# A list scheduler's durations, hand-over delays and two new rules, in a planned network kernel on one core

## The chip, the cores and the metric

The kernel runs on one core of a Trainium2 chip. The metric is the device time of one execution in microseconds. Engine names in the profile: PE is TensorE's matmuls and PEld its weight loads, DVE is VectorE, ACT is ScalarE, POOL is GpSimd, SP is SyncE, whose queue issues most loads.

## The reference, cut to what matters

A network of three layers on 512 tokens of width 1024, with a context of 256 tokens in the first two. A layer of the first block:

```python
mx = jnp.split((jax.nn.silu(c) @ w_ada[l] + b_ada[l])[:, None, :], 6, axis=-1)
hx = modulate(rmsnorm(x, g_pre_mix[l]), mx[0], mx[1])
hc = modulate(rmsnorm(ctx, g_pre_mix[l]), mc[0], mc[1])
out_x, out_c = token_mixers(hx, hc, w_in[l], w_out[l], ...)
x = x + mx[2] * rmsnorm(out_x, g_post_mix[l])
hx = modulate(rmsnorm(x, g_pre_mlp[l]), mx[3], mx[4])
x = x + mx[5] * rmsnorm(sq_relu_mlp(hx, w_mlp1[l], w_mlp2[l]), g_post_mlp[l])
```

`token_mixers` runs a chunked mLSTM in both directions, a Fourier mixer and a convolution module side by side; `sq_relu_mlp` is `jnp.square(jax.nn.relu(h @ w1)) @ w2` with a hidden width of 4096. Context tokens take the same way in layer 0. A third layer with sparse attention, pooling and a memory follows. All is float32.

## The kernel before, in words

Activations stand with channels on the partitions and tokens in the columns: 768 columns in layer 0 (tiles of 512 and 256), 512 in layer 1. A float32 product is made of three fast ones: the weights are split into a rounded high part `wh` (ScalarE, from the raw weights `wr`) and the rest `wl` (VectorE), the activations likewise, and TensorE adds high*high, high*low and low*high in a PSUM tile `pd`. Weights stream from HBM in blocks of 512 KB. `w_ada`, which gives the modulation vectors, goes straight from `wr` through small products into `pa`. The MLP uses Strassen's scheme for most of its products: `combos` (line 1270) makes sums and differences T1 to T4 of the quarters of the activations, on VectorE and POOL, as `tmp`; `fast` (line 1486) uses them, `plain` (line 1479) does a tile without them, and `product2` (line 1475) is the second matrix. A hidden tile is squared by `square_parts` (line 1439): ScalarE takes relu into `ftmp` and the square's rounded part into a `slot`, POOL the full square into `ftmp`, and VectorE subtracts, `slot<-ftmp,slot`, for the low part. In layer 0 the program is `plain` for four column blocks, `combos`, then `product2` and `fast` in turn, seven times.

The program does not issue instructions itself. It is written to a `Recorder` (class at line 136), which notes each one with its engine, operands and dependences. All of them appear in the profile on one line, L395 in `issue`, so a tile's name tells what an instruction is. `schedule` (line 247) then goes through a model of time. An engine that is free takes, of the instructions that are ready, the one written first (some are marked urgent by a number), if its buffers can be had. Buffers are rings: 23 of `slot`, 6 of `tmp`, 4 of `ftmp`, 3 of `wr`, 2 each of `wh` and `wl`, 3 of `pd`, 4 of `pm`, 1 of `pa`. How long an instruction takes in the model is told by `cost` (line 212), and when the next may follow by constants in `schedule`:

```python
SEM, SLACK, SAME = 120.0, 300.0, {"pe": 0.0, "act": 120.0, "vec": 130.0, "pool": 60.0, "sp": 0.0}
...
wait = SAME[e] if same else SEM + (SLACK if ops[j].eng == "pe" else 0)
ready_at[j] = max(ready_at[j], o.end + wait)
```

The result is one fixed order for each engine and each queue. On the chip an engine runs its order strictly: an instruction that has to wait keeps back all that stands behind it on that engine, and a load on SP that waits for its buffer keeps back the loads behind it.

## Time and profile before

| | |
|---|---|
| median of 3 runs | 1974.14 us (1968.65 to 1974.84) |
| profiled execution, its own time | 1975.36 us |
| its span, first to last instruction | 1973.6 us |
| mean granted TensorE clock | 0.98 |
| TensorE busy | 1890.9 us, 96% |
| VectorE busy | 1354.0 us, 69% |
| ScalarE busy | 908.9 us, 46% |
| POOL busy | 425.8 us, 22% |

Busy shares are means over stages with different limits. Since TensorE is busy nearly always, the table says little more than where not to look; what a change of order can alter is in the few stretches in which TensorE stands still, and there the rows by time tell which engine it waited for. In those rows a number in brackets is the idle time just before an instruction and the engine and tile that ended it. Several equal instructions in a row are told as one with a count.

### The profile page before, as it was taken

What the parts mean: (1) busy time and instruction counts of PE and PEld (TensorE: products, weight loads), DVE (VectorE), ACT (ScalarE), POOL (GpSimd) and SP (SyncE); (2) the same over time, 40 slices, a digit from 0 to 9 for tenths busy, and PEclk for the clock granted to TensorE, in tenths of its full rate; (3) what the DMA queues carried; (4) which work ended last, traced back from release to release, by engine and by line L of the source; (5) the groups of instructions that cost most, each with busy time, mean ns of one, the idle gap of its engine ahead of it and who ended that gap; (6) DMA issues with size and microseconds to landing.
All of it is one profiled execution on the core that took longest, in us unless ns stands there. A gap on an engine that the chain in (4) does not pass through costs nothing.

```text
span 1973.6 us, 32415 instructions
## 1 busy us (share of the span) xinstructions
PE 1890.9 (96%) x12772; PEld 1641.0 (83%) x12772; DVE 1354.0 (69%) x2370; ACT 908.9 (46%) x1786; POOL 425.8 (22%) x438
## 2 busy tenths in 40 slices
PE   5999998998999999999989999889999999999999
PEld 3978886787888999999978888778989889888777
DVE  6499768368356556665677968577787778657686
ACT  4532256564323322332573345655334347556554
POOL 1110042215112211221301023233232221111321
PEclk8999999898999999999999999899999999999999
DMA  8233235243233112211361123352323244311121
GB/s 312 90 110 108 96 109 177 68 150 107 96 118 126 65 56 75 76 65 54 108 216 68 54 86 140 107 171 81 112 86 116 98 137 162 109 54 44 46 84 65
DMA packets 82714, 207.47 MB, mean 105 GB/s; under 512 B 8961, under 2 KB 36865, under 8 KB 82562
## 3 DMA queue, kind: packets, MB, share of 16 engines
q1 hardware_dynamic: 66114, 188.86, 28.0%
q10 hardware_dynamic: 16448, 16.54, 2.5%
q8 instruction: 100, 1.64, 0.3%
q14 instruction: 52, 0.43, 0.1%
HBM read 189.12 MB, written 16.25 MB: 104 GB/s over the span
## 4 chain that ended last, share of the span: by engine, by line
PE 80%; DVE 11%; ACT 3%; DMA 2%; issue 2%; POOL 1%; SPq 0%; DVEq 0%; POOLq 0%; ACTq 0%
PE pd L395 57%; PE pm L395 21%; DVE slot L395 7%; PE pa L395 3%; DVE tmp L395 2%; ACT slot L395 1%; DVE wl L395 1%; DMA wr<-in_w_ada 1%; DVE small L395 1%; ACT tmp L395 1%; DMA wr<-in_w_in 1%; ACT small L395 1%; DMA slot<-in_w_ada 1%; ACT wh L395 0%; DVE ftmp L395 0%
## 5 line engine op out<-in xcount | busy, mean ns | idle before, releaser
L395 PE MATMUL pd<-slot,wh 128*128 128x256 f32 (+2 forms) x4384 | 1092.2, 340 | 14.5 <-DVE slot L395 5.5
L395 PEld LDWEIGHTS pd<-slot,wh 128*128 128x128 f32 (+1 forms) x4384 | 744.7, 189 | 122.0 <-issue 17.5
L395 PE MATMUL pd<-slot,wl 128*128 128x256 f32 (+1 forms) x2136 | 720.9, 339 | 4.9 <-DVE wl L395 4.7
L395 PEld LDWEIGHTS pd<-slot,wl 128*128 128x128 f32 x2136 | 406.8, 191 | 52.1 <-DVE wl L395 6.8
L395 ACT ACTIVATE wh<-wr 128x1024 fp32r<-128x1024 f32 (+2 forms) x202 | 204.9, 1015 | 387.4 <-PE pd L395 356.3
L395 DVE TENSOR_TENSOR wl<-wr,wh 128x1024 fp32r<-128x1024 f32 (+2 forms) x199 | 244.7, 1230 | 128.5 <-ACT wh L395 126.3
L395 PE MATMUL pm<-slot,slot 128*128 128x256 f32 (+3 forms) x1674 | 238.0, 291 | 6.9 <-ACT slot L395 4.0
L395 PEld LDWEIGHTS pm<-slot,slot 128*128 128x128 f32 x1674 | 213.2, 191 | 19.7 <-issue 6.4
L395 DVE TENSOR_TENSOR slot<-pd,slot 128x512 f32<-128x512 f32 (+1 forms) x208 | 119.5, 574 | 122.3 <-PE pd L395 120.4
L395 PE MATMUL pd<-slot,slot 128*128 128x256 f32 (+1 forms) x1048 | 143.0, 285 | 2.4 <-ACT ftmp L395 1.6
L395 PEld LDWEIGHTS pd<-slot,slot 128*128 128x128 f32 x1048 | 130.1, 189 | 8.4 <-issue 3.5
L395 ACT ACTIVATE tmp<-tmp 128x512 f32<-128x512 f32 (+3 forms) x122 | 62.2, 545 | 123.1 <-DVE tmp L395 122.1
L395 DVE TENSOR_TENSOR slot<-ftmp,slot 128x512 fp32r<-128x512 f32 (+2 forms) x116 | 90.9, 786 | 36.5 <-POOL ftmp L395 35.0
L395 DVE SCALAR_TENSOR_TENSOR slot<-slot,const,slot 128x512 f32<-128x512 f32 (+2 forms) x184 | 113.5, 664 | 0.8
L395 POOL TENSOR_TENSOR ftmp<-tmp 128x512 f32<-128x512 f32 x54 | 58.8, 1110 | 214.1 <-ACT tmp L395 214.0
L395 POOL TENSOR_TENSOR ftmp<-ftmp 128x256 f32<-128x256 f32 (+1 forms) x72 | 62.4, 867 | 186.5 <-ACT ftmp L395 154.8
L395 POOL TENSOR_TENSOR wr<-wr 128x512 f32<-128x512 f32 x27 | 39.3, 1456 | 286.4 <-DVE wl L395 247.2
L395 DVE TENSOR_TENSOR slot<-wr,slot 128x512 fp32r<-128x512 f32 (+1 forms) x85 | 86.0, 1018 | 20.8 <-ACT slot L395 20.8
L395 PE MATMUL pm<-slot,wh 128*128 128x256 f32 x544 | 98.4, 281 | 0.0
L395 ACT ACTIVATE slot<-wr 128x512 fp32r<-128x512 f32 (+1 forms) x85 | 72.1, 854 | 44.1 <-POOL wr L395 22.6
L395 ACT ACTIVATE slot<-tmp 128x512 fp32r<-128x512 f32 (+1 forms) x122 | 73.5, 627 | 31.5 <-DVE tmp L395 18.8
L395 PEld LDWEIGHTS pm<-slot,wh 128*128 128x128 f32 x544 | 84.2, 188 | 2.8 <-issue 1.6
(202 smaller groups left out, 2355.3 us busy)
## 6 DMA issues: line engine op xcount, KB each, us to landing
wr<-in_w_mlp SPq DMA_DIRECT2D x128, 512.0 KB, 3.4
wr<-in_w_ada SPq DMA_DIRECT2D x80, 512.0 KB, 3.8
wr<-in_w_in SPq DMA_DIRECT2D x66, 512.0 KB, 3.3
dram<-slot ACTq DMA_DIRECT2D x52, 256.0 KB, 3.3
tmp<-dram SPq DMA_DIRECT2D x40, 256.0 KB, 3.6
slot<-in_w_ada SPq DMA_DIRECT2D x16, 512.0 KB, 9.3
wr<-in_w_out SPq DMA_DIRECT2D x16, 512.0 KB, 4.1
wr<-in_w_out SPq DMA_DIRECT2D x8, 384.0 KB, 2.9
```

The lines of the kernel that those rows point to most:

```text
L395: o.fn(*[conv(x) for x in o.a], **{k: conv(x) for k, x in o.k.items()})
```

## The change

The numbers of the model are replaced, and two rules are new. In `cost`: TensorE's products get 9% longer at 256 columns (108.7 to 118 ns) and 8% at 512; ScalarE's, VectorE's and POOL's instructions get other offsets and slopes. In `schedule`: a result is handed from engine to engine in 40 ns (205 from TensorE, 420 to TensorE, 80 to POOL) in place of 120, and within ScalarE and VectorE in 35 in place of 120 and 130. A change of TensorE's tile shape costs 170 ns. An instruction of VectorE with two SBUF inputs that starts while such a one runs on POOL is made longer by 0.6 of the overlap. No instruction is added or removed; orders and places of buffers change.

```diff
--- before.py
+++ after.py
 
 
 class Op:
-    __slots__ = ("eng", "fn", "method", "a", "k", "deps", "out", "n", "prio", "bufs", "start", "end", "cost", "dma")
+    __slots__ = ("eng", "fn", "method", "a", "k", "deps", "out", "n", "prio", "bufs", "start", "end", "cost", "dma", "mode", "shared")
 
 
 class Recorder:
             return math.prod(x.shape) * 4 / 330
         n = max(out.idx.size, max((v.idx.size for v in op.a if isinstance(v, View)), default=0))
         if op.eng == "pe":
+            lhs = op.a[1]
+            k = lhs.p1 - lhs.p0
+            op.mode = tuple(32 if x <= 32 else 64 if x <= 64 else 128 for x in (k, lhs.idx.size if op.method == "transpose" else lhs.shape[1]))
             if op.method == "transpose":
                 return 110
-            lhs = op.a[1]
             n = out.idx.size
             if lhs.dtype == F32R:
-                return n / 2.4 + 2 if n >= 256 else 107
+                return n * 0.4453 + 4 if n >= 256 else 112
             if lhs.dtype == BF:
-                return max(n / 2.4, 61)
-            c = max(4 * n / 2.4, 217)
-            return c / 4 + 26 if lhs.shape[1] <= 32 else c / 2 if lhs.shape[1] <= 64 else c
+                return max(n / 2.4 + 2.5, 61)
+            c = max(4 * n / 2.4 + 5, 219)
+            return c / 4 + 2 if op.mode == (128, 32) else c / 2 if op.mode == (128, 64) else c
         ins = [v for v in list(op.a[1:]) + [op.k.get("in_"), op.k.get("in0")] if isinstance(v, View)]
         psum = any(v.buf.kind in PSUM_KINDS for v in ins)
+        op.shared = len(ins) > 1 and not psum
         if op.eng == "act":
-            ap = sum(isinstance(op.k.get(x), View) for x in ("bias", "scale"))
-            return (55 if psum else 97) + 0.833 * n + 93 * ap + (93 if "accum_out" in op.k else 0)
+            ap = any(isinstance(op.k.get(x), View) for x in ("bias", "scale"))
+            return (150 + 0.86 * n if psum else 190 + 0.847 * n) + 97 * ap + (195 if op.k.get("accum_out") is not None else 0)
         if op.eng == "vec":
             if op.method == "reciprocal":
-                return 70 + 8 * n
+                return 137 + 8 * n
             if op.method in ("tensor_copy", "tensor_scalar", "memset") and not psum:
-                return 70 + 0.55 * n + (120 if op.method == "tensor_scalar" else 0)
-            return (135 if op.method == "scalar_tensor_tensor" else 70) + 1.042 * n
+                return (200 if op.method == "tensor_scalar" else 150) + 0.65 * n
+            return (200 if op.method == "scalar_tensor_tensor" else 140) + 1.06 * n
         if op.method == "tensor_tensor":
-            return 150 + 2.1 * n
+            return 200 + 2.1 * n
         if op.method == "tensor_scalar":
-            return 200 + 3.6 * n
-        return 100 + 0.85 * n
+            return 350 + 2.8 * n
+        return 110 + 0.85 * n
 
     def schedule(self):
 
                 push(i, 0.0)
         done = 0
         now = 0.0
-        SEM, SLACK, SAME = 120.0, 300.0, {"pe": 0.0, "act": 120.0, "vec": 130.0, "pool": 60.0, "sp": 0.0}
+
+        SAME = {"pe": 0.0, "act": 35.0, "vec": 35.0, "pool": 70.0, "sp": 0.0}
+        SEM, TO = {"pe": 205.0}, {"pe": 420.0, "pool": 80.0}
+        SWITCH, mode = 170.0, None
+        reads = {"vec": 0.0, "pool": 0.0}
         releases = []
 
         def place(o):
                     o.end = dma_free[e] + 1900
                 else:
                     engs[e] = o.end = now + o.cost
+                    if e == "pe":
+                        if mode != o.mode:
+                            engs[e] = o.end = o.end + SWITCH
+                        mode = o.mode
+                    elif e in reads and o.shared:
+
+                        if e == "vec" and reads["pool"] > now:
+                            engs[e] = o.end = o.end + 0.6 * min(reads["pool"] - now, o.cost)
+                        reads[e] = o.end
                 order.append(pick)
                 done += 1
                 for b in o.bufs:
                     b.left -= 1
                     b.end = max(b.end, o.end)
                     if b.left == 0 and self.kinds[b.kind][0] is not None:
-                        heapq.heappush(free[b.kind], (b.end + SEM, b.place))
-                        heapq.heappush(releases, b.end + SEM)
+                        heapq.heappush(free[b.kind], (b.end + 120.0, b.place))
+                        heapq.heappush(releases, b.end + 120.0)
                 for j in succ[pick]:
                     same = ops[j].eng == e and not o.dma
-                    wait = SAME[e] if same else SEM + (SLACK if ops[j].eng == "pe" else 0)
+                    wait = SAME[e] if same else max(SEM.get(e, 40.0), TO.get(ops[j].eng, 0.0))
                     ready_at[j] = max(ready_at[j], o.end + wait)
                     need[j] -= 1
                     if need[j] == 0:
```

VectorE in the first hidden layer of layer 0 (about 475 to 487 us in the trace). `slot<-ftmp,slot` is the low part of a squared hidden tile; `tmp<-...` and `slot<-tmp,slot` belong to T1 to T4; `wl` is the low part of a weight of the product that follows. Before:

```order
L395 TENSOR_TENSOR slot_680_4465<-ftmp_699_4601,slot_680_4465 128x256
L395 TENSOR_TENSOR slot_698_4591<-tmp_692_4549,slot_698_4591 128x512
L395 TENSOR_TENSOR tmp_693_4551<-tmp_693_4551,slot_610_4054 128x512
L395 TENSOR_TENSOR slot_683_4491<-ftmp_703_4631,slot_683_4491 128x256
L395 TENSOR_TENSOR tmp_705_4650<-slot_623_4139,tmp_693_4551 128x512
L395 TENSOR_TENSOR tmp_705_4650<-tmp_705_4650,slot_626_4148 128x512
L395 TENSOR_TENSOR slot_688_4520<-ftmp_706_4661,slot_688_4520 128x256
L395 TENSOR_TENSOR wl_710_4683<-wr_665_4387,wh_709_4668 128x1024
L395 TENSOR_TENSOR slot_610_4054<-tmp_693_4551,slot_608_4044 128x512
L395 TENSOR_TENSOR slot_694_4556<-ftmp_712_4692,slot_694_4556 128x256
```

Now:

```order
L411 TENSOR_TENSOR slot_679_4463<-ftmp_695_4563,slot_679_4463 128x256
L411 TENSOR_TENSOR slot_623_4133<-tmp_673_4435,slot_619_4123 128x512
L411 TENSOR_TENSOR tmp_694_4558<-tmp_694_4558,slot_615_4090 128x512
L411 TENSOR_TENSOR slot_683_4484<-ftmp_698_4591,slot_683_4484 128x256
L411 TENSOR_TENSOR slot_687_4506<-ftmp_700_4605,slot_687_4506 128x256
L411 TENSOR_TENSOR slot_606_4035<-tmp_680_4465,slot_605_4028 128x512
L411 TENSOR_TENSOR slot_696_4575<-tmp_694_4558,slot_696_4575 128x512
L411 TENSOR_TENSOR slot_690_4540<-ftmp_704_4635,slot_690_4540 128x256
L411 TENSOR_TENSOR slot_707_4660<-tmp_681_4469,slot_696_4575 128x512
L411 TENSOR_TENSOR tmp_708_4668<-slot_608_4047 128x512
L411 TENSOR_TENSOR wl_711_4679<-wr_664_4382,wh_706_4658 128x1024
L411 TENSOR_TENSOR slot_679_4463<-ftmp_712_4687,slot_679_4463 128x256
```

Both pieces begin at the same low part. Before, the `wl` and the fourth low part came after the chain on `tmp_693` and `tmp_705`, the second pair of quarters; now they come when that chain (`tmp_708` here) has only begun, and a fifth low part stands ahead of the rest of it.

VectorE in layer 1, at the same point of the program (about 1318 to 1328 us). Before:

```order
L395 TENSOR_TENSOR slot_1855_12789<-tmp_1889_13009,slot_1854_12779 128x512
L395 TENSOR_TENSOR tmp_1914_13154<-slot_1860_12815,slot_1854_12779 128x512
L395 TENSOR_TENSOR slot_1863_12826<-tmp_1912_13127,slot_1860_12815 128x512
L395 TENSOR_TENSOR tmp_1914_13154<-tmp_1914_13154,slot_1863_12826 128x512
L395 TENSOR_TENSOR tmp_1914_13154<-tmp_1914_13154,slot_1855_12789 128x512
L395 TENSOR_TENSOR wl_1919_13192<-wr_1884_12978,wh_1915_13167 128x1024
L395 TENSOR_TENSOR slot_1898_13043<-ftmp_1918_13188,slot_1898_13043 128x256
L395 TENSOR_TENSOR wl_1923_13216<-wr_1886_12990,wh_1917_13185 128x1024
L395 TENSOR_TENSOR slot_1903_13070<-ftmp_1925_13222,slot_1898_13043 128x256
```

Now:

```order
L411 TENSOR_TENSOR tmp_1912_13152<-tmp_1912_13152,slot_1850_12759 128x512
L411 TENSOR_TENSOR tmp_1915_13175<-slot_1861_12816,slot_1854_12784 128x512
L411 TENSOR_TENSOR wl_1918_13190<-wr_1883_12977,wh_1913_13163 128x1024
L411 TENSOR_TENSOR slot_1895_13036<-ftmp_1919_13194,slot_1895_13036 128x256
L411 TENSOR_TENSOR wl_1924_13219<-wr_1886_12985,wh_1917_13184 128x1024
L411 TENSOR_TENSOR slot_1904_13074<-ftmp_1925_13222,slot_1895_13036 128x256
L411 TENSOR_TENSOR slot_1904_13074<-ftmp_1927_13233,slot_1904_13074 128x256
L411 TENSOR_TENSOR slot_1863_12824<-tmp_1912_13152,slot_1861_12816 128x512
L411 TENSOR_TENSOR tmp_1915_13175<-tmp_1915_13175,slot_1863_12824 128x512
```

The first `wl` stood behind three instructions on `tmp` and `slot<-tmp` that now stand behind it, with three low parts and a second `wl` ahead of them as well.

SP's loads around the state updates of the mLSTM of layer 1 (about 1167 to 1224 us). `in_w_ada` and `in_w_out` are weights into the ring `wr`; `in_ohr` are two small tables from which ScalarE and POOL make an operand of the scores. Before:

```order
L395 DMA wr_1619_11490<-in_w_ada 128x1024
L395 DMA wr_1629_11543<-in_w_ada 128x1024
L395 DMA wr_1639_11600<-in_w_ada 128x1024
L395 DMA tmp_1674_11751<-in_ohr 128x512
L395 DMA tmp_1675_11756<-in_ohr 128x512
L395 DMA tmp_1678_11770<-dram_136_812 128x2x256
L395 DMA tmp_1680_11778<-dram_136_812 128x2x256
L395 DMA tmp_1682_11787<-dram_136_812 128x2x256
L395 DMA tmp_1683_11789<-dram_136_812 128x2x256
L395 DMA wr_1687_11816<-in_w_ada 128x1024
L395 DMA wr_1688_11822<-in_w_ada 128x1024
L395 DMA wr_1690_11830<-in_w_ada 128x1024
```

Now:

```order
L411 DMA wr_1618_11484<-in_w_ada 128x1024
L411 DMA wr_1626_11535<-in_w_ada 128x1024
L411 DMA wr_1635_11590<-in_w_ada 128x1024
L411 DMA wr_1648_11678<-in_w_ada 128x1024
L411 DMA wr_1650_11685<-in_w_ada 128x1024
L411 DMA wr_1659_11717<-in_w_ada 128x1024
L411 DMA wr_1666_11746<-in_w_ada 128x1024
L411 DMA wr_1673_11775<-in_w_ada 128x1024
L411 DMA wr_1678_11795<-in_w_out 128x1024
L411 DMA tmp_1680_11800<-in_ohr 128x512
L411 DMA tmp_1684_11812<-in_ohr 128x512
```

Five loads of `w_ada` and the first of `w_out` moved ahead of the two tables. On TensorE the state updates (`pm<-tmp,slot`, 128x129), which lay between the last projection's products, now come after them, with the products of the `w_ada` blocks between them; on ScalarE the high part of that `w_out` block comes ahead of the two copies of the tables.

## Rows read from the trace of the kernel before

**Rows 1.** The page: busy time of each engine, share of the span, instructions.
```profile
PE 1890.9 (96%) x12772; PEld 1641.0 (83%) x12772; DVE 1354.0 (69%) x2370; ACT 908.9 (46%) x1786; POOL 425.8 (22%) x438
```

**Rows 2.** Stretches: window; us, then busy us (count) of five engines, granted clock, DMA.
```profile
455.00:491.00 36.00, 31.59 (x234) 29.25 (x232) 35.42 (x43) 20.40 (x46) 25.89 (x21) 0.95 0.16 52
491.00:500.00 9.00, 9.00 (x45) 7.12 (x45) 1.29 (x2) 2.31 (x4) 0.00 (x0) 0.81 0.10 36
1314.00:1345.00 31.00, 25.32 (x177) 23.56 (x177) 29.63 (x29) 14.96 (x30) 23.23 (x18) 0.94 0.15 51
1345.00:1355.00 10.00, 10.00 (x58) 8.68 (x57) 5.99 (x8) 5.63 (x9) 2.60 (x2) 1.00 0.16 54
...
420.00:455.00 35.00, 28.01 (x191) 20.66 (x190) 24.28 (x39) 18.59 (x36) 2.12 (x2) 0.80 0.72 249
976.00:1030.00 54.00, 47.16 (x346) 39.93 (x348) 43.02 (x77) 39.73 (x79) 5.15 (x6) 0.94 0.61 204
...
487.60:494.40 6.80, 6.08 (x18) 4.85 (x19) 2.96 (x10) 2.47 (x6) 1.57 (x2) 0.50 0.23 78
1327.30:1330.70 3.40, 3.40 (x18) 3.40 (x17) 3.40 (x5) 0.00 (x0) 2.86 (x3) 0.50 0.68 228
```

**Rows 3.** TensorE by time, 470 to 489: start, us, instruction, [idle before, what ended it].
```profile
475.93 3.11 PE L395 MATMUL pd<-slot,slot 128*128 128x256 f32 x24 [1.63 <-ACT ftmp L395]
...
488.32 0.58 PE L395 MATMUL pd<-slot,wh 128*128 128x256 f32 x1 [2.23 <-DVE slot L395]
```

**Rows 4.** VectorE by time, 474 to 491.
```profile
473.35 1.77 DVE L395 TENSOR_TENSOR slot<-tmp,slot 128x512 fp32r<-128x512 f32 x1
...
475.38 0.68 DVE L395 TENSOR_TENSOR slot<-tmp,slot 128x512 fp32r<-128x512 f32 x1
...
487.86 0.41 DVE L395 TENSOR_TENSOR slot<-ftmp,slot 128x256 fp32r<-128x256 f32 x1
```

**Rows 5.** POOL by time, 455 to 491.
```profile
472.84 1.72 POOL L395 TENSOR_TENSOR tmp<-tmp,slot 128x512 f32<-128x512 f32 x1
```

**Rows 6.** VectorE's groups by form, 455 to 491: count, busy us, mean ns.
```profile
L395 DVE TENSOR_TENSOR slot<-ftmp,slot 128x256 fp32r<-128x256 f32 x12 | 9.1, 759 | 0.5 <-ACT ftmp L395 0.5
```

**Rows 7.** TensorE by time, 1313 to 1329.
```profile
1316.44 0.38 PE L395 MATMUL pd<-slot,wh 128*128 128x256 f32 x1 [0.92 <-DVE slot L395]
...
1326.99 0.39 PE L395 MATMUL pd<-slot,wl 128*128 128x256 f32 x1 [3.38 <-DVE wl L395]
```

**Rows 8.** VectorE by time, 1316 to 1330.
```profile
1325.31 1.63 DVE L395 TENSOR_TENSOR wl<-wr,wh 128x1024 fp32r<-128x1024 f32 x1
```

**Rows 9.** TensorE by time, in three places between 1183 and 1217.
```profile
1183.70 1.05 PE L395 MATMUL pm<-tmp,slot 128*128 128x129 f32 x8
1184.51 0.71 PE L395 MATMUL pd<-slot,wh 128*128 128x512 f32 x2
...
1200.04 0.74 PE L395 MATMUL pd<-slot,slot 104*128 104x512 f32 x2
...
1215.56 0.64 PE L395 MATMUL pa<-wr,const 128*32 128x256 f32 x8
```

**Rows 10.** DMA issues: KB each, median us from issue to landing.
```profile
wr<-in_w_out SPq DMA_DIRECT2D x16, 512.0 KB, 4.1
...
tmp<-in_ohr SPq DMA_DIRECT2D x4, 256.0 KB, 2.6
```

**Rows 11.** The page: ScalarE's group of high parts of weights.
```profile
L395 ACT ACTIVATE wh<-wr 128x1024 fp32r<-128x1024 f32 (+2 forms) x202 | 204.9, 1015 | 387.4 <-PE pd L395 356.3
```

**Rows 12.** All engines by time, 1195 to 1198, two instructions of them.
```profile
1195.18 0.63 ACT L395 ACTIVATE slot<-tmp 128x512 fp32r<-128x512 f32 x1 [8.25 <-DMA tmp<-in_ohr]
...
1195.89 1.03 POOL L395 TENSOR_TENSOR slot<-slot,const 8x512 fp32r<-8x512 f32 x1 [2.13 <-ACT slot L395]
```

**Rows 13.** What TensorE waits for: us in total, times, longest us.
```profile
PE pm L395 <- DVE tmp L395: 11.0, 11, 4.4
PE pm L395 <- DVE slot L395: 10.0, 10, 2.9
```

## The prediction

> **What bounds the kernel now.** I read the busy times first, then the busy time of each engine by stretch, then the list of what TensorE waits for, then the order of instructions on single engines where it waits. TensorE is busy for 1890.9 us of a span of 1973.6 [rows 1]: 82.7 us is all its idle time, so no change of order can gain much more than that, plus what the clock gives back. The idle time lies in a few stages, each a chain from engine to engine; in most of the 50 us stretches between them TensorE has no gap. What the reader is to see in the stretches [rows 2] is a pair. In 455 to 491 VectorE is busy for 35.42 of 36.00 us and TensorE for 31.59: there VectorE is the bound. In the 9 us that follow VectorE works 1.29 us. The same happens a layer later: 29.63 of 31.00 us, then 5.99 of 10.00.
>
> Profiled time 1975.4 us, against which the sum is made; the median of the runs is 1974.1, 0.06% less. About 0.3%, 5.9 us, is what a measurement of this kernel can tell from no change.
>
> **The change part by part.** No instruction is added or removed; the planner's numbers change, and with them the order on all engines. Each cost below is one of a moved instruction.
>
> *First hidden layer of layer 0 (455 to 491).* The 12 hidden tiles each need a chain TensorE, ScalarE, POOL (the square), VectorE (its low part, slot<-ftmp). Between them stand the differences of the Strassen quarters, on POOL and VectorE, which are used only after the whole next product, over 20 us later. TensorE waits 1.63 us for a buffer of that chain, then 2.23 us for a low part [rows 3]. The new order puts the low parts and the first wl ahead of the differences, on POOL too. Of what stands ahead of the low part that ends the 2.23 us wait (it ended at 488.27 [rows 4]), nine VectorE instructions go behind it, each 0.68 to 1.8 us like the two shown, some 8.6 us in all. So the waits go: 1.63 + 2.23 = 3.9 us. The moved differences run after 491, beside TensorE, in the 7.7 us that VectorE has idle there [rows 2]; if that cover were gone, they would cost what they save. From 487.6 to 494.4 the granted clock was 0.50, the level of 1.2 GHz, after those waits; 6.08 us of matmuls there are about 3.0 us at 2.4 GHz [rows 2]. If the waits go, so does this: together **-6.9**.
>
> One price there is contested. A 128x512 difference of two SBUF tiles takes VectorE 0.68 us alone and 1.77 us when it begins 0.5 us after a POOL one of 1.72 us has begun [rows 4, 5]: it ends 0.56 us after POOL's. The change charges 0.6 of the overlap, at most 0.41 us for such an instruction, so its plan still has VectorE too early by up to 0.7 us each. I price with the durations of the rows, in which this is contained for the old pairs; the new pairs can be worse. With five more such pairs ahead of the low parts, 5 x 1.1 = 5.5 us, the 8.6 us still hold.
> The Trainium skill ("SBUF — State Buffer", section "SBUF: two separate sides") says of VectorE with two SBUF inputs and GpSimd that the one that starts second blocks fully until the first is done. The end of VectorE's instruction behind POOL's agrees with it. By that, with a POOL instruction in front of each of the 12 low parts, they would take 12 x 1.1 = 13.2 us more than alone where they took 4.2 us more (mean 0.76 [rows 6], 0.41 alone); these 9.0 us use up the 8.6, the 2.23 us and the clock stay lost, the stage gains an estimated 1.7 us and the sum below would be -5.5.
>
> *The same place in layer 1 (1314 to 1345).* Waits of 0.92 and 3.38 us [rows 7]. The last is for a wl that ran 1325.31 to 1326.94 [rows 8] behind three differences; in the new order its wh stands ahead of a copy on ScalarE, and it stands ahead of three differences on VectorE. So 4.3 us go, and 3.4 us at a clock of 0.50 [rows 2], worth 1.7: **-6.0**.
>
> *State updates of layer 1 (from 1183).* Before, the 40 small matmuls were laid between those of the projection. Now the projection ends first, at about 1188, and the updates have only w_ada matmuls between them, whose loads are pulled forward: five more loads and the first one of w_out now stand on SP ahead of the two small loads (tmp<-in_ohr) that scores need. The ring of raw weights has three places, so the w_out load waits until the sixth w_ada load has been used. I count to there: from 1183.7 the last 21 matmuls of the projection at 0.22 to 0.23 give 1188.4; then scores' four 1.0, 28 small ones at 0.22 (four with the changeover in 0.81 us), six groups of w_ada at 0.5 (alone 0.64 of busy time) [rows 9]: 1198.6. The small loads land 2.6 us later, but ScalarE has the wh of w_out first in its order: load 4.1 us [rows 10], 1.0 us of work [rows 11], then two copies of 0.63 and POOL's second 1.03 [rows 12]: about 1206.5. TensorE is there, at the matmul of 1200.04 before [rows 9], after 12 more small ones and two groups, by about 1202.4: a wait of 4.1 us that was none. Bounds: nothing if the w_out load comes with the small ones; 8 us with the clock dropped as well. Against it the last two chunks' chains of ScalarE interleave better, -1.2 us, and I add 0.6 for the clock: **+3.5**.
>
> *Other chains.* Here a wh, 1.0 us on ScalarE [rows 11], is now ahead of a link of the chain that TensorE waits for, and more matmuls stand in front of the wait.
> - 420 to 455: 22 matmuls, 2.6 us, fill the wait of 4.4 us [rows 13]; the chain becomes 2.4 us longer by a wh and two splits: **0**; bounds -2.6 and +2.4.
> - 976 to 1030: 26 matmuls fill 3.1 us, the chain is longer by up to 4, and w_ada loads issued earlier on SP may save 2: **-1**; bounds -5 and +3.
> - 339 to 358: the wh and its wl go ahead of squares, +1.8, an earlier output -1.1: **+0.7**; bounds -1 and +1.8.
> - Convolution inputs at 145 and 1092: eight matmuls of 256 columns or four of 512, 0.9 us, fill each wait, one of them 2.9 us [rows 13]: **-2**; bounds -5 with the clock, and 0.
> - Start: a wl goes ahead of the modulation's gains and a sum goes behind 11 more matmuls; no row shows it, and I take the mean wait of [rows 13], 1.0 us: **+1**; bounds 0 and 3.
> - Changes of TensorE's tile shape, which the plan now charges: counted in the orders they are 215 and 219, so nothing.
> - Waits that I did not find, one of 1.0 us [rows 13], against shorter ones than those shown, in the two stages above, that go too: **0**; bounds -1 and the second rival.
>
> Sum: -6.9 - 6.0 + 3.5 + 0 - 1 + 0.7 - 2 + 1 + 0 = -10.7, so 1964.7, **1965 us**, 0.5% less.
>
> **The rivals.**
> 1. *The gain is given back (no difference).* The wh ahead of a chain's link costs its upper bound where it moved: 420 to 455 +2.4, 339 to 358 +1.1 more than above, 976 to 1030 +4 more, and the state updates 3 more: +10.5, and the time is 1975.2. For it: all these chains end in waits of TensorE already, and two of their stretches have it busy for 28.01 of 35.00 and 47.16 of 54.00 us [rows 2]. Against it: ScalarE has 16.4 and 14.3 us free in these two, so a wh often fits into a gap. A quarter.
> 2. *Slower.* The plan now takes 40 ns from engine to engine in place of 120, and 35 in place of 120 to 130 on one engine. In the 14 steps of the two Strassen MLPs, where TensorE now has no gap, it puts VectorE's and ScalarE's instructions closer. If each step gets a wait before each of its two wl, of the mean 1.0 us of [rows 13], that is 28 us: 1965 + 28 = 1993. It decides from 17 such waits, since 10.7 + 5.9 has to be made up. Against it: VectorE is idle for 7.7 of 9 us after 491, so a wl has slack there. One in nine.
> 3. *More is gained.* The waits in state updates, start and elsewhere don't come (-3.5 - 1 - 0.7 = -5.2), and the stretches 420 to 455 and 976 to 1030, at a clock of 0.80 and 0.94, get back half of what it cost: a share of 0.20 below full is 0.20 x 35 = 7 us, and 0.06 x 54 = 3.2, half of which is 5.1. That is 1954. One in eight.
> 4. That the change does little is excluded: the orders printed differ in all the places named.
>
> **How the numbers follow.** My forecast, 1965 with a range of its own of 1959 to 1968, has 0.52; rival 1 0.25, rival 2 0.11, rival 3 0.12. Faster is the forecast and rival 3: 0.64; same 0.25; slower 0.11. The range of 8 in 10 goes from 1953 (most of rival 3) to 1978 (rival 1 with its spread), and leaves out rival 2 and the end of 3.
>
> **What would show it.** Right: TensorE's waits for slot and wl in 455 to 491 and 1314 to 1345 are gone, and its busy time there comes near the whole stretch; VectorE's differences run after it; no clock of 0.50 behind either. Before the scores of layer 1 there is a new wait of 3 to 5 us that ends with POOL. Wrong: waits of the same length stand in the next product (the differences were needed after all), or new waits for wl in the Strassen steps.

## The result, and the profile after

The changed kernel takes 1991.86 us (median of 4 runs, 1989.74 to 1994.38), before on the same chip 1973.14 (4 runs, 1968.65 to 1974.84): a ratio of 1.0091, interval 1.0075 to 1.0107. It is 0.9% slower; the forecast was 0.5% faster. The profiled execution took 1994.38 us with a span of 1992.6. Times below are medians; one of e7's four executions, 2345.92 us at a granted clock of 0.745, is left out of its median.

The busy line of the page, to be laid beside [rows 1]:

```profile
PE 1897.1 (95%) x12772; PEld 1646.3 (83%) x12772; DVE 1364.1 (68%) x2370; ACT 910.6 (46%) x1786; POOL 434.9 (22%) x438
```

The span grew by 19.0 us, TensorE's busy time by 6.2 for the same 12772 matmuls. So 12.8 us are more idle time, and 6.2 are matmuls at the lower clock: the granted clock was 1.2 GHz for 94.3 us in place of 81.7, and half of the 12.6 us more is 6.3.

What TensorE waits for, the whole run (us in total, times, longest us):

```profile
PE pm L411 <- ACT slot L411: 12.9, 5, 6.8
PE pa L411 <- DMA slot<-in_w_ada: 12.4, 3, 11.5
PE pd L411 <- ACT slot L411: 10.9, 5, 4.6
PE pm L411 <- DVE tmp L411: 8.8, 5, 3.6
...
PE pd L411 <- DVE wl L411: 7.1, 7, 4.1
PE pd L411 <- DVE slot L411: 7.0, 7, 5.2
PE pd L411 <- POOL slot L411: 6.4, 3, 3.7
```

The two groups of [rows 13] did shrink (tmp 11.0 to 8.8; slot, 10.0 before, is 4.8 now), but longer waits stand elsewhere. To find where, I looked up each TensorE instruction in both traces and took, by stretch, the median of how much later it starts in the changed kernel. The growth of this shift over a place is what the place cost. Times of the first column are those of before. Each kernel's shift is read from one execution, and those of before differ by up to 6 us among themselves, so a cost of 1 or 2 us says little.

```
place                                  cost, us   predicted
start, to 130                            +0.2       +1
130 to 262 (convolution, layer 0)        -2.9       } -2
1080 to 1190 (convolution, layer 1)      -2.4       }
262 to 335 (state updates, layer 0)      +7.1        0
335 to 420                               +2.0       +0.7
420 to 455                               -0.2        0
455 to 500 (first hidden layer, l. 0)    -3.4       -6.9
500 to 990 (Strassen steps, layer 0)     +0.2        0
990 to 1080                              -2.5       -1
1190 to 1290 (state updates, layer 1)   +16.7       +3.5
1290 to 1310                             -0.5        -
1310 to 1400 (first hidden layer, l. 1)  +1.4       -6.0
1400 to 1740 (Strassen steps, layer 1)   -0.3        0
1740 to 1860 (third layer)               +3.7        0
rest                                     -0.2        -
```

The sum is 18.9, and 19.0 without rounding. One stretch makes most of it. Here are four places in the changed kernel, cut so that they hold the same work, but for one or two matmuls, as the windows of before under them (window; length, busy us and count of PE, PEld, DVE, ACT, POOL; granted clock; DMA share; GB/s): first hidden layer of layer 0, state updates of layer 0 and of layer 1, first hidden layer of layer 1.

```profile
461.20:499.80 38.60, 36.09 (x260) 33.51 (x259) 37.54 (x43) 21.69 (x48) 27.82 (x22) 0.96 0.15 54
257.30:329.40 72.10, 61.88 (x494) 50.99 (x493) 52.35 (x145) 32.88 (x84) 30.47 (x29) 0.93 0.35 122
1181.10:1261.80 80.70, 63.62 (x425) 51.29 (x424) 53.86 (x161) 38.01 (x106) 26.49 (x24) 0.85 0.24 86
1320.00:1359.50 39.50, 33.52 (x249) 30.46 (x250) 37.03 (x44) 22.12 (x48) 27.13 (x22) 0.93 0.25 87
```

The same in the kernel before:

```profile
455.00:497.00 42.00, 37.59 (x259) 34.31 (x258) 35.49 (x43) 21.38 (x48) 25.89 (x21) 0.92 0.14 45
260.00:325.00 65.00, 59.51 (x492) 49.04 (x491) 49.91 (x142) 32.20 (x84) 30.34 (x29) 0.97 0.37 127
1183.00:1247.00 64.00, 56.63 (x424) 46.38 (x423) 49.51 (x157) 38.59 (x104) 23.05 (x20) 0.92 0.30 108
1306.00:1345.00 39.00, 33.32 (x249) 30.67 (x242) 36.32 (x42) 22.70 (x49) 27.09 (x22) 0.96 0.23 83
```

Length less busy time is idle time. In the third row of each, TensorE's idle time goes from 7.4 to 17.1 us and its busy time for the same matmuls from 56.6 to 63.6, at a clock of 0.85 in place of 0.92: 9.7 + 7.0 = 16.7. In the first row idle time falls from 4.4 to 2.5 and busy time by 1.5: that is the gain of 3.4.

TensorE by time in layer 1's state updates, the changed kernel, three of the long waits:

```profile
1206.06 0.51 PE L411 MATMUL pd<-slot,slot 104*128 104x512 f32 x1 [3.74 <-POOL slot L411]
...
1226.95 0.47 PE L411 MATMUL pd<-slot,slot 104*128 104x512 f32 x1 [2.89 <-DVE small L411]
...
1251.92 0.86 PE L411 MATMUL pm<-const,slot 128*128 128x128 f32 x2 [6.80 <-ACT slot L411]
```

The first of them is the wait that was forecast, 4.1 us at about 1206.5, ended by POOL. The other two were not.

### The profile page after: what moved, and what is told of

It is laid out like the page before. It is cut to its first block, busy times and chain, and to the rows that moved or that the text cites. A ratio compares the mean times of both kernels' runs of the same rounds, so it can differ in the third digit from the quotient of the medians.

```text
span 1992.6 us, 32444 instructions
## 1 busy us (share of the span) xinstructions
PE 1897.1 (95%) x12772; PEld 1646.3 (83%) x12772; DVE 1364.1 (68%) x2370; ACT 910.6 (46%) x1786; POOL 434.9 (22%) x438
## 4 chain that ended last, share of the span: by engine, by line
PE 66%; DVE 5%; DMA 2%; ACT 1%; issue 1%; POOL 1%; DVEq 0%; POOLq 0%; ACTq 0%
PE pd L411 46%; PE pm L411 18%; DVE slot L411 3%; PE pa L411 2%; DMA wr<-in_w_ada 1%; DVE tmp L411 1%; DVE wl L411 1%; ACT slot L411 1%; DVE small L411 0%; DMA wr<-in_w_out 0%; POOL slot L411 0%; ACT wh L411 0%; DMA wr<-in_w_in 0%; POOL ftmp L411 0%; ACT small L411 0%
## 5 line engine op out<-in xcount | busy, mean ns | idle before, releaser
L411 PE MATMUL pd<-slot,wh 128*128 128x256 f32 (+2 forms) x4384 | 1090.1, 340 | 12.6 <-ACT slot L411 9.2
L411 PE MATMUL pd<-slot,slot 128*128 128x256 f32 (+1 forms) x1048 | 148.3, 288 | 17.5 <-POOL slot L411 6.4
L411 DVE TENSOR_TENSOR slot<-ftmp,slot 128x512 fp32r<-128x512 f32 (+2 forms) x116 | 101.5, 880 | 43.2 <-POOL ftmp L411 42.0
L411 POOL TENSOR_TENSOR ftmp<-ftmp 128x256 f32<-128x256 f32 (+1 forms) x72 | 75.5, 1050 | 216.8 <-ACT ftmp L411 160.0
L411 DVE SCALAR_TENSOR_TENSOR slot<-slot,const,slot 128x512 f32<-128x512 f32 (+1 forms) x184 | 112.7, 664 | 0.8
L411 DVE TENSOR_TENSOR slot<-wr,slot 128x512 fp32r<-128x512 f32 (+1 forms) x85 | 90.3, 1064 | 21.3 <-ACT slot L411 21.1
L411 POOL TENSOR_TENSOR wr<-wr 128x512 f32<-128x512 f32 x27 | 34.9, 1291 | 285.0 <-DVE wl L411 235.2
```

The lines of the kernel that those rows point to most:

```text
L411: o.fn(*[conv(x) for x in o.a], **{k: conv(x) for k, x in o.k.items()})
```

## The experiments

**Which of the parts does it.** Four runs take one part of the change out or put one alone into the kernel before.

e1 is the changed kernel with the old hand-over delays.

```diff
-SEM, TO = {"pe": 205.0}, {"pe": 420.0, "pool": 80.0}
+SEM, SLACK, SAME = 120.0, 300.0, {"pe": 0.0, "act": 120.0, "vec": 130.0, "pool": 60.0, "sp": 0.0}
```

> The changed kernel with the hand-over delays of before (120 us/1000 from engine to engine, 300 more to TensorE, 120 to 130 within an engine); durations, tile-shape cost and overlap rule stay changed. In its order 28 of the 40 state-update matmuls of layer 1 lie again ahead of the end of the projection, and only three w_ada loads stand ahead of the small tables. Theory A, the shorter delays make the loss of layer 1's mLSTM (17 us in the trace of the change, from 1172 to 1247 of before): the time falls by 12 to 17 us, to 1975 to 1980, and no wait of TensorE for POOL of over 1 us stands before the scores of layer 1. Rival B, the new durations make it: 1987 or more. Rival C, any new order of this planner is about as bad: within 4 us of 1992.

Measured 1985.17 us, ratio to before 1.0081 (1.0059 to 1.0102): between the ranges of the three theories. In the place of the state updates of layer 1 it still loses 12.6 us.

e2 is the kernel before with only the new delays (the same lines the other way round).

> The kernel before with the new hand-over delays alone. Its order has 4 of the 40 state updates ahead of the end of the projection and six loads ahead of the small tables, but none of VectorE's low parts of layer 0 and two of the three places in layer 1 gained. Theory A: slower than before by 6 to 17 us, 1979 to 1990, the loss in layer 1's mLSTM. Rival B: within 5 us of before, 1968 to 1978.

Measured 1988.11, ratio 1.0087 (1.0069 to 1.0106). Alone the delays cost nearly what the whole change costs, and without them it still costs 0.8%: the parts don't add up.

e6 is the kernel before with only the new `cost`, of which a few lines stand here:

```diff
-return n / 2.4 + 2 if n >= 256 else 107
+return n * 0.4453 + 4 if n >= 256 else 112
...
-return (55 if psum else 97) + 0.833 * n + 93 * ap + (93 if "accum_out" in op.k else 0)
+return (150 + 0.86 * n if psum else 190 + 0.847 * n) + 97 * ap + (195 if op.k.get("accum_out") is not None else 0)
...
-return (135 if op.method == "scalar_tensor_tensor" else 70) + 1.042 * n
+return (200 if op.method == "scalar_tensor_tensor" else 140) + 1.06 * n
```

> The kernel before with the new durations alone. Its order has 28 of the 40 state updates ahead of the projection's end, the tables where they were, the sum of layer 0's mLSTM behind the four stretched instructions, and neither gain at the MLPs' starts in full (four of nine, none of three). Theory A, durations cost in both mLSTMs what the first experiment still lost there: 5 to 13 us slower than before, 1977 to 1985. Rival, durations taken from the trace do no harm by themselves: within 4 us of before.

Measured 2001.23, ratio 1.014 (1.0124 to 1.0157): worse than the whole change, and a miss. Most of the loss, 20.8 us, lies in the state updates of layer 0 (262 to 335), where the whole change lost 7.1.

e7 is the changed kernel without the charge for TensorE's shape.

```diff
-SWITCH, mode = 170.0, None
+SWITCH, mode = 0.0, None
```

> The changed kernel without the 170 ns for a change of TensorE's tile shape. Its order keeps the state updates behind the projection and all nine loads ahead of the tables; the sum of layer 0's mLSTM is not moved behind the stretched instructions. Theory A: 5 us less than the change (layer 0), 1985 to 1989, the loss of layer 1 unchanged. Rival, the charge keeps w_ada's products apart from the rest and so is the cause in layer 1: 1980 or less.

Measured 1994.02, ratio 1.0109 (1.0089 to 1.013): a miss. The loss of layer 1 stays, 16.0 us, and that of layer 0 grows from 7.1 to 12.7. The shape charge is not the cause.

**POOL's effect on VectorE.** e3 is the kernel before with only that rule, e8 the same with the whole rest of POOL's instruction charged.

```diff
+engs[e] = o.end = o.end + 0.6 * min(reads["pool"] - now, o.cost)    (e3)
+engs[e] = o.end = o.end + (reads["pool"] - now)                     (e8)
```

> The kernel before with the overlap rule alone (VectorE lengthened by 0.6 of its overlap with POOL). Its order has the low parts ahead of the quarters' differences in both layers (eight of nine in layer 0, three of three in layer 1), the state updates and tables where they were before, and the sums of the mLSTM of layer 0 not moved. Theory A, the gains forecast for these two places are real and independent of the rest: 7 to 13 us faster than before, 1960 to 1966. Rival: what is gained there is lost a few microseconds later, since VectorE's work is only moved: within 3 us of before, 1970 to 1976.

Measured 1969.90, ratio 0.9996 (0.998 to 1.0011): no difference.

> The kernel before with an overlap rule alone, and a stricter one: a VectorE instruction with two SBUF inputs that starts while such a one runs on POOL ends later by all that is left of POOL's. Low parts and wl stand first at both MLP starts (nine of nine, three of three). Theory A, the rows show the full block, so the plan fits better than with 0.6 of the overlap: 2 to 6 us faster than before, 1966 to 1970, and faster than the third experiment. Rival: the same as before within 3 us.

Measured 1967.53, ratio 0.9977 (0.9964 to 0.9991): 0.2% faster than before, the best kernel of this study. What it does to the first hidden layer of layer 0 can be read from one row (455 to 500 of its own time, same columns as above; the work of 455 to 497 of before runs there from 449.8 to 483.7, and TensorE has no wait in the rest of it either):

```profile
455.00:500.00 45.00, 45.00 (x316) 40.29 (x315) 29.21 (x38) 21.72 (x44) 21.01 (x18) 1.00 0.22 71
```

TensorE is busy for all 45 us, at full clock: the two waits of [rows 3] are gone. The matched shift falls by some 8 us from 455 to 500, where the forecast had 6.9 and the change brought 3.4; in e3 it falls by 5.3. So the gain was there to be had, with a plan that knows the whole price of an overlap. The intervals of e3 and e8 overlap, so that the whole rest is the better charge than 0.6 is shown for this stretch, not for the time.

**The loads of the tables.** e4 takes away the cause that the prediction named for layer 1: the two small loads and their copies are written inside the state updates, at the fourth of the five steps, and so in front of the loads that kept them back.

```diff
+    if step == 3:
+        Rt = slot([P, 2, 4, P], F32R)
+        for d in range(2):
+            t = tmp([P, 4, P])
+            ld(t, A["ohr"][:, d])
+            A_(Rt[:, d], t, AF.Copy)
```

> The changed kernel with the two small tables of the scores (tmp<-in_ohr) and their copies written two steps of the state updates earlier in the program; nothing else. Two of the w_ada loads and the w_out load then stand behind the tables on SP, and the w_out high part behind both copies on ScalarE. Theory A, the late tables cause the waits of 3.7 and 0.6 us for POOL in layer 1 and of 2.0 us in layer 0, and the clock of 0.50 after them: 5 to 9 us faster than the change, 1983 to 1987. Rival, the chain behind was late anyway for lack of matmuls between: the wait goes but the time stays within 3 us of 1992.

Measured 1984.47, ratio 1.0071 (1.0056 to 1.0086), 7.4 us less than the changed kernel (5.9 if each is taken against the runs of before beside it), as expected, but not where expected. In layer 0 the place from 262 to 335 costs 0.2 where it was 7.1: the wait of 2.02 us for POOL shown below is gone. In layer 1 the wait for POOL is gone and the place still costs 14.2 us. TensorE by time there:

```profile
1211.54 0.77 PE L411 MATMUL pd<-slot,slot 104*128 104x512 f32 x1 [3.51 <-DVE small L411]
...
1237.09 0.33 PE L411 MATMUL pm<-const,slot 128*128 128x128 f32 x1 [2.75 <-ACT slot L411]
...
1241.50 0.86 PE L411 MATMUL pm<-const,slot 128*128 128x128 f32 x2 [2.78 <-ACT slot L411]
...
1245.91 0.86 PE L411 MATMUL pm<-const,slot 128*128 128x128 f32 x2 [2.28 <-ACT slot L411]
```

The late load was one wait of a chain that is short of other matmuls; with it gone, the next links wait.

**The token mixers planned as before.** e5 is the changed kernel in which all instructions of the token mixers of layers 0 and 1 are planned with the old numbers.

```diff
+        need = l == 0
+        rec.old = l in (0, 1)
...
+        if op.old:
+            op.cost = self.cost_old(op, outs[0] if outs else None)
```

> The changed kernel, but the instructions of the token mixers of both layers (mLSTM, Fourier, convolution and the w_ada steps between them) are planned with all the numbers of before; the rest with the changed ones. In its order the mixers' places are those of before (all 40 state updates ahead of the projection's end, three loads ahead of the tables, the sum of the mLSTM of layer 0 not moved), the low parts and wl of the MLPs' starts those of the change. Theory A, the loss is made in the mixers (24 to 27 us in the trace of the change: 7.5 before 335, 2.5 at 355, 17 from 1190 to 1290), the MLP starts are a small gain: 1965 to 1971. Rival B, TensorE's work is a chain of stages and a loss saved here returns as soon as a stage lacks matmuls: 1976 or more.

Measured 1972.27, ratio 0.9993 (0.9983 to 1.0002): the time of before, just above the range of theory A. With the mixers' order of before the whole loss is gone. The rest of the changed numbers gains 3 us from 455 to 500 and 4 from 990 to 1080, and gives it back, half of it in the third layer.

**Is it the numbers, or any other order?** e9, e10 and e11 put the new durations of one group of engines alone into the kernel before: of the lines shown for e6 the first pair is in e9 (TensorE), the second in e10 (ScalarE), the third in e11 (VectorE, and POOL's with it).

> The kernel before with only TensorE's new durations in the plan; ScalarE's, VectorE's and POOL's are the old ones. All new durations together took 28.6 us more than before. Theory A (the higher figures of VectorE and POOL are what turns the mixers' order, since these engines carry the chains there): this one stays within 6 us of before, 1966 to 1979. Rival B (any change of a duration re-deals the mixers' order, and most deals are worse than the old one): 5 to 15 us more, 1977 to 1988. Rival C (ScalarE's figures do it): as A here.

Measured 1986.31, ratio 1.0069 (1.0046 to 1.0093), as rival B had it, but not in the mixers' state updates: 5.9 us are lost in the Strassen steps from 500 to 990, and 6.7 in the third layer.

> The kernel before with only ScalarE's new durations in the plan (some 95 ns more for each of its instructions, 195 in place of 93 for an accumulated one). Theory A (VectorE's and POOL's figures do it): within 6 us of before, 1966 to 1979. Rival B (every re-deal is worse): 1977 to 1988. Rival C (ScalarE's figures do it, as its instructions are links of every chain of the mixers): 15 us or more above before, from 1987.

Measured 2002.81, ratio 1.0158 (1.0128 to 1.0189).

> The kernel before with only VectorE's and POOL's new durations in the plan (70 ns more for most of VectorE's, 50 to 150 for POOL's). Theory A: most of the 28.6 us of all new durations, 1988 to 2003, with long waits of TensorE for VectorE between 262 and 335 us and at 1190 to 1250. Rival B (every re-deal is worse, by about as much): 1977 to 1988. Rival C (ScalarE's): 1966 to 1979.

Measured 2010.51, ratio 1.0192 (1.0167 to 1.0218). Each part alone is slower, and their sum is far over what all of them do. So I gave the planner numbers that mean nothing (e13 to e15): each duration of before up to 6% off, by a fixed rule of which only one constant differs.

```diff
+        if not op.dma:
+            op.cost *= 1 + 0.006 * ((int(op.cost) * 7919 // 13 + len(name)) % 21 - 10)
```

> The kernel before with meaningless numbers: each duration in the plan is made up to 6% longer or shorter by a fixed rule that has nothing to do with the chip. It moves about as many instructions as the new delays do (350 of VectorE's against 352, 227 of ScalarE's against 227). Theory A (the new numbers themselves push the order the wrong way): noise costs little, within 6 us of before, 1968 to 1980. Rival B (the order of before is a good deal among many, and any other deal costs): 7 to 25 us more, 1981 to 1999.

Measured 1981.06, ratio 1.0042 (1.0029 to 1.0055).

> As the first noise, by another fixed rule. Theory A: 1968 to 1980. Rival B: 1981 to 1999. If the three noises differ among themselves by as much as the single parts of the change do (over 15 us), a part's own time says little of whether its numbers are right.

Measured 1990.78, ratio 1.0094 (1.0077 to 1.0111).

> As the first noise, by a third rule. Theory A: 1968 to 1980. Rival B: 1981 to 1999.

Measured 1985.78, ratio 1.006 (1.0045 to 1.0075). Noise alone costs 8 to 17 us, up to about all that the change costs. In the third one TensorE's waits in layer 1's state updates are those of the changed kernel within 0.2 us:

```profile
1203.79 0.80 PE L397 MATMUL pd<-slot,slot 104*128 104x512 f32 x1 [3.94 <-POOL slot L397]
...
1223.08 0.77 PE L397 MATMUL pd<-slot,slot 104*128 104x512 f32 x1 [2.83 <-DVE small L397]
...
1248.07 0.86 PE L397 MATMUL pm<-const,slot 128*128 128x128 f32 x2 [6.63 <-ACT slot L397]
```

One count of the orders tells these runs apart. The state updates of layer 1 have 40 small matmuls (pm<-tmp,slot). Here is how many of them stand on TensorE ahead of the projection's last matmul, and what the place from 1190 to 1290 costs:

```
ahead of it   kernels                                     cost of the place, us
40 of 40      before, e3, e5, e8, e9, e12, e13, e16, e18   0 to 3.1
28            e1, e6                                      12.6, 9.7
12            e10, e14                                    11.4, 11.4
4             e2                                           9.9
0             changed, e4, e7, e11, e15, e17              14.2 to 17.1
```

All orders with the 40 ahead cost at most 3.1 us there, all others at least 9.7 (among those the cost doesn't follow the count). Which numbers led to an order doesn't matter, whether new, old or noise. Layer 0 shows the same at its ends. Before has 36 of its 40 ahead; the orders with 36 or more cost at most 0.3 us from 262 to 335, those with none (e6, e7, e11) 20.8, 12.7 and 24.0, those between, with 24 to 32, from 0.1 to 7.1. These places are not the whole time: e9 and e13 have all 80 ahead and are 13 and 8 us slower than before.

**Two combinations.** e12 is e5 with VectorE charged the whole rest of POOL's instruction everywhere; e16 charges it outside the mixers alone.

```diff
-engs[e] = o.end = o.end + 0.6 * min(reads["pool"] - now, o.cost)
+engs[e] = o.end = o.end + (reads["pool"] - now)                     (e12, e16)
-elif e in reads and o.shared and not o.old:
+elif e in reads and o.shared:                                       (e12 alone)
```

> The two changes that did no harm so far, together: the changed kernel with the token mixers planned by all old numbers, but with VectorE charged the whole rest of POOL's instruction everywhere (in the mixers too). Theory A (the gains of the mixers planned as before and of the full charge lie in different places and add up): below the full charge alone, 1960 to 1966. Rival (both have the same gain, at the MLPs' starts, and the new numbers cost a little at 1740 to 1800): 1967 to 1973. If the mixers' order turns under the charge as it did under the other terms: from 1975.

Measured 1982.95, ratio 1.0059 (1.004 to 1.0079).

> The changed kernel with the token mixers planned by all old numbers and no charge, and VectorE charged the whole rest of POOL's instruction in the rest of the program. With the charge in the mixers too it took 1983.0; with the smaller charge outside alone 1972.3. If the loss was the charge in the mixers: 1965 to 1973. If it was the charge at the MLPs' starts together with the new numbers there (it lost 10 us from 1310 to 1365): 1978 to 1986.

Measured 1975.58, ratio 1.0013 (1.0002 to 1.0025). Two edits that did no harm alone cost 0.6% together, and in e16 what was won from 455 to 500 (8.0 us by the matched shift) went again from 1290 to 1400 (+6.6) and in the third layer (+5.4). In the first of these TensorE waits 4.15 us for ScalarE, in the way shown for e18 below; why the two edits together lead to such an order is open.

**The wait that moved.** In the changed kernel the wait of 3.38 us for a wl [rows 7] in layer 1's first hidden layer has shrunk to 1.08, and a longer one for the next product's wl has come. VectorE by time, then TensorE:

```profile
1347.76 1.78 DVE L411 TENSOR_TENSOR tmp<-tmp,slot 128x512 f32<-128x512 f32 x1
1349.57 0.99 DVE L411 TENSOR_TENSOR tmp<-slot,tmp 128x512 f32<-128x512 f32 x1
...
1350.82 0.68 DVE L411 TENSOR_TENSOR tmp<-tmp,slot 128x512 f32<-128x512 f32 x1
1351.42 1.28 DVE L411 TENSOR_TENSOR slot<-tmp,slot 128x512 fp32r<-128x512 f32 x2
1352.62 2.28 DVE L411 TENSOR_TENSOR wl<-wr,wh 128x1024 fp32r<-128x1024 f32 x1
```

```profile
1354.96 0.79 PE L411 MATMUL pd<-slot,wl 128*128 128x512 f32 x1 [4.08 <-DVE wl L411]
```

e17 plans this wl ahead of four of the differences; e18 does it in e5.

```diff
+for i in (11345, 11347, 11354, 11355):
+    ops[i].deps = ops[i].deps | {11368}
```

> The changed kernel with one local edit: in layer 1's first hidden layer the wl of the next product (VectorE, 1352.62 in the changed kernel) is planned ahead of four of the differences that stood in front of it. Theory (the wait of 4.08 us at 1355 is the moved wait, and those four differences of some 3 us are its cause): the wl ends about 2.9 us earlier, at 1352, the wait shrinks to about 1.2 us, and with the clock behind it the place gives back 3 to 4.5 us; time 1987 to 1989.5. Rival (VectorE is full there whatever its order, and the differences left behind are waited for next): a wait of TensorE for slot or tmp of 2 to 4 us appears between 1355 and 1375, and the time stays within 1.5 us of the changed kernel's.

Measured 1990.13, ratio 1.0086 (1.007 to 1.0102). The wait shrank as expected, and others came behind it:

```profile
1350.62 0.50 PE L413 MATMUL pd<-slot,wl 128*128 128x512 f32 x1 [1.06 <-DVE wl L413]
1359.30 0.39 PE L413 MATMUL pm<-slot,wl 128*128 128x256 f32 x1 [0.28 <-DVE wl L413]
1361.59 0.73 PE L413 MATMUL pd<-slot,wh 128*128 128x512 f32 x2 [0.73 <-ACT slot L413]
```

The place won 1.0 us of the 3 to 4.5, and the time fell by 1.7: neither of the two expectations came in full.

> The same edit in the changed kernel with its token mixers planned by the old numbers (1972.3 without the edit). Theory: again 3 to 4.5 us less, 1968 to 1969.5: both places that lost are then closed, and it is 3 to 5 us faster than before. Rival: as without it, 1971 to 1974.

Measured 1972.51, ratio 0.9998 (0.9985 to 1.0011), as without the edit: the wait for wl is 0.99 us and one of 2.17 for ScalarE follows. The differences were the cause of that wait, and taking it away gains next to nothing. ScalarE, then TensorE, by time:

```profile
1343.90 0.63 ACT L455 ACTIVATE slot<-tmp 128x512 fp32r<-128x512 f32 x1 [3.92 <-POOL tmp L455]
1344.44 1.55 ACT L455 ACTIVATE slot<-pd 128x512 f32<-128x512 f32 x3
```

```profile
1345.07 0.73 PE L455 MATMUL pd<-slot,wh 128*128 128x512 f32 x2 [2.17 <-ACT slot L455]
```

ScalarE's copies out of `pd` stand in its order behind the high part of a difference, for which it waits for POOL; TensorE goes on when the first copy has ended. The waits of 0.73 us in e17 and of 4.15 us in e16 end in the same way.

## Why the prediction was wrong

**The step that failed is the state updates of layer 1, +3.5 where 16.7 was measured.** The prediction saw the cause in the order ("Now the projection ends first, ... and the updates have only w_ada matmuls between them") and priced one result of it, the late small loads. That wait came at its place and with its size, 3.74 us for 4.1, and was one of several. What was not priced is the loss of the projection's matmuls as cover for the whole chain: the waits of 2.89 and 6.80 us further on, and a clock of 0.85 in place of 0.92 over 81 us. The text set -1.2 us for chunks that "interleave better" there. e4 shows that the loads are not what the place costs, and in the count over 20 orders the 40 ahead and a low cost of the place go together without an exception. That count is no run in which only the interleaving is changed, so it is strong but not a proof; e5, which plans the mixers as before, comes nearest.

**The same in layer 0, 0 where 7.1 was measured.** I had read no place there, and had put the unseen waits at 0. In the changed kernel a wait for the tables' operand stands there that before has not:

```profile
289.28 0.80 PE L411 MATMUL pd<-slot,slot 104*128 104x512 f32 x1 [2.02 <-POOL slot L411]
```

With the tables written earlier (e4) it is gone and the place costs 0.2, while a wait of 5.25 us for VectorE (311.53) stays, as 5.55. So the late tables cause the 7.1, as far as an edit can show it that moves other instructions of the plan too.

**First hidden layer of layer 0: the place right, the size half** (-3.4 for -6.9). The waits of 1.63 and 2.23 us are gone, and shorter ones are left, 2.5 us together. The longest, and ScalarE just before it:

```profile
493.29 0.38 PE L411 MATMUL pd<-slot,wh 128*128 128x256 f32 x1 [1.48 <-ACT slot L411]
```

```profile
492.30 0.63 ACT L411 ACTIVATE slot<-tmp 128x512 fp32r<-128x512 f32 x1 [1.51 <-DVE tmp L411]
492.84 0.40 ACT L411 ACTIVATE slot<-ftmp 128x256 fp32r<-128x256 f32 x1
```

The granted clock was 0.50 for 3.4 us from 494.0, where it was so for 6.8 us before: of the 3.0 us that the clock was to give back, half came. What failed is "So the waits go". The nine VectorE instructions did go behind, but other differences still stood between the low parts, and on ScalarE the rounded part of a square, `slot<-ftmp`, stood behind the high part of a difference, for which ScalarE waited 1.51 us for VectorE. VectorE's low parts from 455 to 500 in the changed kernel (count, busy us, mean ns, idle before):

```profile
L411 DVE TENSOR_TENSOR slot<-ftmp,slot 128x256 fp32r<-128x256 f32 x12 | 10.2, 866 | 0.0
```

A mean of 866 ns where it was 759 [rows 6], and no idle time before them: VectorE was full, busy for 37.54 of 38.60 us. The same 42 instructions of VectorE took 38.2 us before, 39.9 in the changed kernel and 35.2 in e8. So the new pairs with POOL cost 1.7 us, less than the 5.5 that the prediction allowed ("five more such pairs"), and the gain was not whole even so, for VectorE had no time to spare. The Trainium skill ("SBUF — State Buffer", section "SBUF: two separate sides") calls the port pair that VectorE and GpSimd share an exclusive lock, under which the other engine "fully blocks"; by its price the stage gained an estimated 1.7 us. The measured 3.4 lies between that and my 6.9. The three plans that charge by that sentence (e8, e12, e16) gained more than the 6.9 in this stage, 7.6 to 8.4 us; those with 0.6 of the overlap gained 1.5 to 5.3.

**First hidden layer of layer 1: wrong** (+1.4 for -6.0). The waits at 1316 and 1327 shrank, and 4.08 us came in the next product, for the differences that were said to be "used only after the whole next product": these were not needed, but the next wl stood behind them. The prediction named this sign among those that would prove it wrong. What limits there is VectorE, 37.03 busy us in 39.50, and behind it ScalarE's order: e17 and e18 show that another place of the wl only moves the wait.

**The small terms** held within their bounds, or nearly: 420 to 455 -0.2 for 0, 976 to 1030 -2.5 for -1, the convolutions -5.3 for -2, just past their bound of -5, the start +0.2 for +1; 339 to 358 came out at about its upper bound. The third layer's +3.7 was unseen. The granted clock was 0.50 there for 3.4 us from 1770.6, where it was full before, which is 1.7 of it; the rest is not explained.

**The rivals.** Rival 2 gave 1993 for a slower kernel, close to what came, but by waits in the Strassen steps, and these cost nothing (+0.2 and -0.3). Its number was right by accident. What the prediction lacked is a rival that doesn't rest on a place: an order that comes out of a greedy plan is one among many, all single parts that ran, but the rule on POOL, and all three noises made it slower by 0.4 to 1.9%, and the order of before is better than what the planner mostly finds. The chance of 0.64 for faster took new numbers for a better order.

## What to carry to other kernels

Where a greedy list scheduler sets the order, its time under a change of its numbers must be compared with its time under meaningless changes of the same size: here these cost 8 to 17 us, and within that a time does not tell whether the new numbers are right. Look for the few interleavings that carry much of the time (here 40 small matmuls among each projection's) and write them down as constraints, so that no number can undo them (no run here tried that). When a chain loses the work that was laid between its links, price every link to the end of the chain, with the clock, and not only the first that comes late.

## What the runs showed of the hardware

Over the whole run the new waits cost half as much again as their length: 12.8 us more idle time came with 6.2 us more busy time of TensorE for the same matmuls, at a granted clock of 1.2 GHz for 12.6 us more.

Beside POOL, a small instruction of VectorE grew by a larger factor than a 128x512 one: 0.35 to 1.90 us against 0.68 to 1.77 [rows 4]. In layer 0's state updates of the changed kernel (VectorE, then POOL by time):

```profile
305.81 4.97 DVE L411 SCALAR_TENSOR_TENSOR slot<-slot,small 128x128 f32<-128x128 f32 x4
310.71 0.68 DVE L411 TENSOR_TENSOR slot<-slot,pd 128x512 f32<-128x512 f32 x1
```

```profile
305.68 3.64 POOL L411 TENSOR_TENSOR slot<-slot,slot 128x768 fp32r<-128x768 f32 x2 [0.95 <-POOL slot L411]
309.27 1.10 POOL L411 TENSOR_TENSOR slot<-slot,const 8x512 fp32r<-8x512 f32 x1
```

From 255 to 345 such a 128x128 instruction has this minimum, median and maximum (ns):

```profile
L411 DVE SCALAR_TENSOR_TENSOR slot<-slot,small x20: 339/346/1904, 299.8 to 341.7; 128x128 f32<-128x128 f32 x20
```

The four take 4.97 us where 4 x 0.346 = 1.4 would do, and end some 0.4 us after POOL's three. A charge of 0.6 of the overlap, at most 0.6 of the instruction, is 0.2 us each, for up to 1.56.
